# One joined product for four heads, scaling queued behind a split, spaced sums and an interleaved end in a hybrid mLSTM and sparse-attention block

## The chip, the cores and the metric

The kernel runs on one core of a Trainium2 chip. The metric is device time in microseconds (us) of one execution. Five engines have a queue of their own each and work through it in order: TensorE (PE, matrix products; its weight loads are listed apart as PEld), VectorE (DVE), ScalarE (ACT), GpSimd (POOL) and SyncE (SP, which issues most DMA transfers). They wait for each other by semaphores.

## The reference

One layer over 256 tokens of width 4096, batch 1, float32. Cut to what matters:

```python
h = _rmsnorm(x, norm_w)
u = h @ w_in                       # 4096 x about 15,400 columns
# mLSTM: 8 heads, from ml_q ml_k ml_v ml_o ml_z ml_i ml_f     -> y_ml
# sparse attention: 16 query heads in 4 groups of 4           -> y_ns
...
kcmp = _rmsnorm(_compress(kc), k_norm_w[0])     # 15 compressed keys per group
vcmp = _compress(vc)                            # 15 compressed values per group
p_c = _masked_softmax(q @ kcmp * scale + bias_c, dist_c >= 0)
o_c = p_c @ vcmp
o_s = ...   # attention over selected blocks (all 4 blocks of 64 here)
o_w = ...   # attention over a window
o = gs[..., 0:1] * o_c + gs[..., 1:2] * o_s + gs[..., 2:3] * o_w
...
x = x + concat([y_ml, y_ns]) @ w_out
x = x + sigmoid(x @ ple_gate) * (p @ ple_proj)
```

## The kernel before, in words

**Units.** The time goes to four big products with weights of 4096 rows: `w_in` (twice: `wide_group` for most columns, `pair_group` for gates), `w_out` and `ple_gate`. Weights arrive as `raw` tiles of 128x1024 over SP's queue. To keep float32 accuracy, each tile is split in two: ACT writes the high part `whi` (line 1315) and DVE the rest `wlo` (line 1316). PE then makes three products for each block, high by high, high by low and low by high. The work on one `raw` tile is a unit. In a `wide_group` a unit is 12 products of 512 columns (lines 819 and 821). The program's main loop over n emits, for unit n: the split of unit n+3 (`LOOK` = 3; four buffers each for `whi` and `wlo`), loads, PE's products of unit n, and then one step of a generator from the queue `urgent` and one from the queue `fifo`. All other work is written as such generators, so that a piece of it comes after each unit. `require(flag)` runs steps until a flag is set.

**Attention, `t_nq`.** It runs once for each of four groups, under the units of the first stage. After the compressed scores it goes through eight pairs (head h, token half t), one step of the loop to a unit. Three stages stand in a step, for pairs i, i-1 and i-2 and one older: `scores` (lines 489 to 491, PE, into a bank that is written anew in each step), `bias_max` (lines 500 and 502, DVE), `expo` (line 507, ACT), `coef` (lines 512 and 513, DVE), `scale` (line 517, ACT), `trans` (line 524, PE: two transposes where t is 0 and four where t is 1), `copy_pt` (line 529, DVE) and `pv` (line 535, PE). At the end of each `pv` one more product (line 538) adds the compressed branch: 15 rows of `pct` by 15 rows of `vcmp`, at row 32 times the head's number. That is 32 such products in the program.

**Mixed blocks.** `pair_group` has sixteen blocks kp of two `raw` tiles. Most are plain ("C"). Some are mixed: they save a product of eight by adding weights and activations first. The sums of weights are two DVE operations for each tile in `sums` (lines 1140 to 1144), and the sums of activations are made by `t_stat` for blocks 9, 11 and 13 and by `t_mix` (lines 698 to 711) for 3, 5 and 7. `t_mix` is used four times: twice early, and twice behind `t_stat`, in the first group of `w_out` (flag y) and the first group of `ple_gate` (flag r).

**The end.** The last group's four blocks of results (own, 128x512 each) are finished by `t_out_own`, g == 7: an add (line 1012, DVE), a sigmoid (line 1013, ACT), a product and an add (lines 1017 and 1018, DVE) and a DMA. The PE order `tail` lets these blocks be complete one after the other.

Of the kernel before, what the change touches and what calls it, by code (L numbers as in the profile page):

```python
# [13 lines left out]
AF = mybir.ActivationFunctionType  # L14
OP = mybir.AluOpType
# [6 lines left out]
NCMP = 15  # L22
# [51 lines left out]
def hymba_block(ctx: ExitStack, tc: tile.TileContext, a, out: bass.AP):  # L74
    nc = tc.nc
    MM = nc.tensor.matmul
# [14 lines left out]
    def side(i, shape):  # L91
        return psp.tile(shape, F32, tag=f"sd{i}", name=f"sd{i}")
# [4 lines left out]
    def sqtile(shape):  # L97
        return wk.tile(shape, F32, tag="sq", name="sq")

    def stile(shape):  # L100
        return wk.tile(shape, F32, tag="s", name="s", bufs=3)
# [4 lines left out]
    def small(shape, tag, bufs=2):  # L106
        return sm_.tile(shape, F32, tag=tag, name=tag, bufs=bufs)
# [44 lines left out]
    vcmp = wk.tile([128, 4, 128], F32, tag="vcmp", name="vcmp")  # L152
# [7 lines left out]


    fifo, urgent = deque(), deque()
    done = set()

    def step(queues=None):
# [250 lines left out]
    def t_nq(flag, g):  # L416
# [8 lines left out]
        for t in range(2):  # L425
            r = slice(t * 128, (t + 1) * 128)
# [18 lines left out]
        for t in range(2):  # L445
            for h in range(4):
                MM(pc[:, 4 * t + h, :], qt[:, h, t * 128:(t + 1) * 128], kct[:, g, :], start=True, stop=True)
        yield
        sc = small([128, 8, 32], "sc", 1)
        nc.gpsimd.memset(sc, 0.0)  # L450
        scv = sc[:, :, 0:NCMP]
# [16 lines left out]
        for t in range(2):  # L468
            nc.vector.tensor_tensor(scv[:, 4 * t:4 * t + 4], scv[:, 4 * t:4 * t + 4],
                                    mask01[:, t, None, :].to_broadcast([128, 4, NCMP]), op=OP.mult)  # L470
        yield
        pp = side(1, [128, 2, 128])
        for t in range(2):
            nc.tensor.transpose(pp[:, t, :], sc[:, 4 * t:4 * t + 4, :].rearrange("p h c -> p (h c)"), idn)
        yield
        pct = small([128, 2, 128], "pct", 1)
        nc.vector.tensor_copy(pct, pp)

        o = [side(2, [128, 4, 128]), side(3, [128, 4, 128])]
# [51 lines left out]
        def pv(i):  # L531
            h, t = units[i]
            for b in range(2):
                for s in range(t + 1):
                    MM(o[t][:, h, :], ptb[i][:, b, s, :], v[:, s, b, g * 128:(g + 1) * 128],
                       start=(b == 0 and s == 0), stop=False)

            MM(o[t][:, h, :], pct[32 * h:32 * h + NCMP, t, :], vcmp[32 * h:32 * h + NCMP, g, :],
               start=False, stop=True)

        def at(f, i):
            if 0 <= i < 8:
                f(i)

        for i in range(11):
            at(coef, i - 1)
            at(scale, i - 1)
            at(trans, i - 2)
            at(pv, i - 3)
            at(scores, i)  # L550
            at(copy_pt, i - 2)
            at(bias_max, i)
            at(expo, i)
            yield
        if g % 2 == 0:
            nat[2 + g // 2] = wk.tile([128, 2, 1024], F32, tag=f"nat{2 + g // 2}", name=f"y{2 + g // 2}")
        y = nat[2 + g // 2]
# [132 lines left out]
            t = held["cb"][:, int(kp == 11)]  # L690
        return t[:, 0], t[:, 1]

    def t_mix(kps, flag, early=False):

        f = {}
        for i in range(len(kps) + 1):
            if i:
                nc.vector.tensor_sub(cb[kps[i - 1]][1], f[i - 1], cb[kps[i - 1]][0])
                done.add(f"{flag}{kps[i - 1] // 2}m")
            if i == len(kps):  # L700
                return
            c, b = kps[i] // 2, 2 * (kps[i] % 2)
            v = f[i] = stile([128, 4, 128])
            nc.vector.tensor_add(v.rearrange("p a t -> p (a t)"), sh[c][:, b:b + 2].rearrange("p k t -> p (k t)"),
                                 sl[c][:, b:b + 2].rearrange("p k t -> p (k t)"))
            nc.vector.tensor_sub(v[:, 3:0:-2], v[:, 1::-1], v[:, 3:0:-2])
            nc.vector.tensor_sub(v[:, 0], v[:, 0], v[:, 3])
            nc.vector.tensor_sub(v[:, 2], v[:, 2], v[:, 0])
            yield
            cb[kps[i]] = mixed_tiles(kps[i], "a" if early else "b")  # L710
            nc.scalar.activation(cb[kps[i]][0], v, AF.Copy)
            yield

    def t_stat(chunks, weighted, bset=1, pace=2, pause=0):

# [123 lines left out]
    def add(*gens):  # L839
        fifo.extend(gens)  # L840
# [162 lines left out]
    def t_out_own(g, own, us, pj):  # L1003
        while f"mix{g}" not in done:
            yield
        x1 = nat[g - 4]
        if g == 7:
            for j in range(2):
                for t in range(2):
                    cs = (slice(0, 256), slice(256, 512)) if t and j else (slice(0, 512),)  # L1010
                    for c in cs:
                        nc.vector.tensor_add(us[j][:, t, c], own[t][j].t[:, c], us[j][:, t, c])  # L1012
                        nc.scalar.activation(us[j][:, t, c], us[j][:, t, c], AF.Sigmoid)  # L1013
                    for c in cs:
                        w, c0 = us[j][:, t, c], 512 - 512 * j + c.start
                        n = c.stop - c.start
                        nc.vector.tensor_tensor(w, w, pj[:, j, t, c], op=OP.mult)  # L1017
                        nc.vector.tensor_add(w, w, x1[:, t, c0:c0 + n])  # L1018
                        nc.sync.dma_start(out[t * 128:(t + 1) * 128, 3072 + c0:3072 + c0 + n], w)
            done.add("own7")  # L1020
            return
        for j in range(2):
            for t in range(2):
                nc.vector.tensor_add(us[j][:, t], own[t][j].t, us[j][:, t])
        done.add(f"own{g}")
        yield
        for j in range(2):
            u = us[j]
            nc.scalar.activation(u, u, AF.Sigmoid)
            nc.vector.tensor_tensor(u, u, pj[:, j], op=OP.mult)  # L1030
            yield
            c0 = 512 - 512 * j
            nc.vector.tensor_add(u, u, x1[:, :, c0:c0 + 512])
            nc.gpsimd.dma_start(out[:, (g - 4) * 1024 + c0:(g - 4) * 1024 + c0 + 512].rearrange("(t p) c -> p t c", p=128), u)
            yield
# [31 lines left out]
    def pair_group(g, w, stat):  # L1067
# [3 lines left out]
        own = [[Acc(6 * nC + (0 if (t, j) == (1, 0) else 3 * nM)) for j in range(2)] for t in range(2)]  # L1071
        oth = [Acc(3 * nM) for _ in range(4)]
        us, pj, raw, left, tail = [], {}, {}, {c: 2 for c in range(8)}, []
# [33 lines left out]
        def new_activations(g, chunks, b):  # L1107

            if g < 0:
                add(t_stat([(c, (c * 512 + 2048) % 4096, f"p1_{c}", f"y{c}") for c in chunks], range(16), b, pause=2 - 2 * b))  # L1110
            else:
                add(t_stat([(c, c * 512, f"p2_{c}", f"r{c}") for c in chunks], (), b, pause=2 - 2 * b))
            if b:
                add(t_mix((3, 5, 7), "y" if g < 0 else "r"))

        def finish(kp):
            if g in (-1, 3):
# [191 lines left out]
    def split_tiles():  # L1309
        return (wk.tile([128, 2, 512], F32R, tag="whi", name="whi", bufs=LOOK + 1),  # L1310
                wk.tile([128, 2, 512], F32R, tag="wlo", name="wlo", bufs=LOOK + 1))

    def split_all(r, keep=False):
        hi, lo = split_tiles()
        nc.scalar.activation(hi, r, AF.Copy)  # L1315
        nc.vector.tensor_sub(lo, r, hi)  # L1316
        held_raw[0] -= not keep
        return hi, lo
# [7 lines left out]
    def split(n):  # L1326
        r = raws.pop(n, None)
        if n == 0:
            hi, lo = split_tiles()
            for j in range(2):  # L1330
                split_x(j)
                nc.scalar.activation(hi[:, j], r[:, j], AF.Copy)
                nc.vector.tensor_sub(lo[:, j], r[:, j], hi[:, j])
            splits[n] = (hi, lo)
            held_raw[0] -= 1
            return
        if n < 16:
            split_x(2 * n)
            split_x(2 * n + 1)
        if n - 1 in XN:  # L1340
            done.add(f"xn{XN.index(n - 1)}")
        if units[n]["kind"] == "raw":
            splits[n] = (r, None)
        elif units[n]["kind"] == "narrow":
            hl = wk.tile([128, 8, 128], F32R, tag="whi", name="whl", bufs=LOOK + 1)
            nc.scalar.activation(hl[:, :, 0:64], r, AF.Copy)
            nc.vector.tensor_sub(hl[:, :, 64:128], r, hl[:, :, 0:64])
            splits[n] = (hl, None)
            held_raw[0] -= 1
        elif units[n]["kind"] == "pair":  # L1350
            splits[n] = units[n]["split"](r)
        else:
            splits[n] = split_all(r)
# [4 lines left out]
    def load_some():  # L1358
        while loads and held_raw[0] < RAWB:
            held_raw[0] += 1  # L1360
            load(loads.popleft())
# [6 lines left out]
    for n in range(N):  # L1368
        if n + LOOK < N:
            split(n + LOOK)  # L1370
        load_some()
        un = units[n]
        if un["pre"]:
            un["pre"]()
        un["mm"](*splits.pop(n))
        if un["kind"] == "raw":
            held_raw[0] -= 1
        if un["post"]:
            un["post"]()
        if n >= 3:  # L1380
            step([urgent])
            step([fifo])
# [85 lines left out]
```

## Time and profile before

| | |
|---|---|
| median of 3 runs | 2169.69 us (2169.62 to 2169.72) |
| the profiled execution | 2169.9 us, of which span 2168.1 us |
| PE | 2146.1 us busy, 99% of the span |
| PEld | 1756.3 us, 81% |
| DVE | 1565.5 us, 72% |
| ACT | 1152.1 us, 53% |
| POOL | 32.1 us, 1% |
| mean granted clock of TensorE | 0.999 |

The span runs from the first to the last instruction, and the profiled execution takes 1.8 us more than it. Shares are of the whole span. A busy PE may still be late: a product is counted as busy until its result has left the array, so the starts of products following each other are the finer measure. A float32 product appears as two MATMUL records, a transpose and a product of split parts as one.

### The profile page before, as it was taken

To read this page: it belongs to the slowest core of one execution; us is meant where nothing else is said; L and a number is where in the kernel's file an instruction comes from. 1 tells how busy PE (TensorE), PEld (TensorE's weight loads), DVE (VectorE), ACT (ScalarE), POOL (GpSimd) and SP (SyncE) were. 2 spreads that over 40 slices of the span, in tenths; PEclk is the share of its full clock that TensorE was granted. 3 is DMA by queue.
4 is the path that set the end of the run, shared out by engine and by line. 5 is a ranking of instruction groups with operands and counts; after the bars stand their busy time and mean duration, and the time that the engine had idled before them with its cause. 6 is when DMAs were issued, how large, how long until landed. Compare 5 with 4: busy or idle time off the path is not lost. (4 is left out here: it accounts for less than half of the span.)

```text
span 2168.1 us, 26804 instructions
## 1 busy us (share of the span) xinstructions
PE 2146.1 (99%) x9795; PEld 1756.3 (81%) x9795; DVE 1565.5 (72%) x1971; ACT 1152.1 (53%) x1462; POOL 32.1 (1%) x70
## 2 busy tenths in 40 slices
PE   9999999999999999999999999999999999999998
PEld 7876888787878788888888888887888888888887
DVE  6553555555555576658888888887898886888888
ACT  7543443545455555455555555565555555555554
POOL 1000000000000000000000000000000000000000
PEclk9999999999999999999999999999999999999999
DMA  9667665464645455655666666666675675666664
GB/s 380 200 196 264 192 188 181 127 186 127 186 133 166 139 184 173 195 167 193 185 196 224 183 200 213 197 204 218 205 229 180 202 226 160 205 196 223 204 217 141
DMA packets 118244, 422.08 MB, mean 195 GB/s; under 512 B 13650, under 2 KB 13962, under 8 KB 118112
## 3 DMA queue, kind: packets, MB, share of 16 engines
q1 hardware_dynamic: 114272, 409.00, 58.9%
q0 software_dynamic: 3696, 11.35, 1.7%
q8 instruction: 77, 1.26, 0.2%
q14 instruction: 55, 0.45, 0.1%
q10 hardware_dynamic: 144, 0.02, 0.0%
HBM read 416.08 MB, written 4.23 MB: 194 GB/s over the span
## 5 line engine op out<-in xcount | busy, mean ns | idle before, releaser
L1316 DVE TENSOR_TENSOR wlo<-raw,whi 128x1024 fp32r<-128x1024 f32 x818 | 998.0, 1223 | 537.3 <-ACT whi L1315 522.8
L1315 ACT ACTIVATE whi<-raw 128x1024 fp32r<-128x1024 f32 x818 | 863.4, 1060 | 789.2 <-PE mm L819 261.5
L819 PE MATMUL mm<-whi,sh 128*128 128x512 f32 x1152 | 362.3, 396 | 0.2 <-ACT whi L1315 0.2
L819 PE MATMUL mm<-whi,sl 128*128 128x512 f32 x1152 | 355.5, 390 | 0.0
L821 PE MATMUL mm<-wlo,sh 128*128 128x512 f32 x1152 | 355.4, 390 | 0.1
L821 PEld LDWEIGHTS mm<-wlo,sh 128*128 128x128 f32 x1152 | 216.1, 188 | 46.3 <-DVE wlo L1316 0.7
L819 PEld LDWEIGHTS mm<-whi,sl 128*128 128x128 f32 x1152 | 216.3, 188 | 46.0
L819 PEld LDWEIGHTS mm<-whi,sh 128*128 128x128 f32 x1152 | 210.6, 188 | 48.3 <-issue 5.9
L1064 PE MATMUL mm<-whi,sh 128*128 128x512 f32 x740 | 239.6, 392 | 2.5 <-DVE sl L759 1.9
L1064 PE MATMUL mm<-wlo,sh 128*128 128x512 f32 x740 | 237.1, 390 | 1.6 <-DVE wlo L1316 1.6
L1064 PE MATMUL mm<-whi,sl 128*128 128x512 f32 x740 | 236.9, 390 | 0.0
L1064 PE MATMUL sd<-whi,sh 128*128 128x512 f32 x677 | 219.8, 390 | 0.0
L1064 PE MATMUL sd<-whi,sl 128*128 128x512 f32 x677 | 219.4, 389 | 0.0
L1064 PE MATMUL sd<-wlo,sh 128*128 128x512 f32 x677 | 219.3, 389 | 0.0
L1064 PEld LDWEIGHTS mm<-wlo,sh 128*128 128x128 f32 x740 | 138.8, 188 | 31.1 <-DVE wlo L1316 2.2
L1064 PEld LDWEIGHTS mm<-whi,sh 128*128 128x128 f32 x740 | 137.8, 188 | 32.0 <-issue 3.5
L1064 PEld LDWEIGHTS mm<-whi,sl 128*128 128x128 f32 x740 | 139.0, 188 | 29.1
L1064 PEld LDWEIGHTS sd<-whi,sl 128*128 128x128 f32 x677 | 127.2, 188 | 26.6
L1064 PEld LDWEIGHTS sd<-wlo,sh 128*128 128x128 f32 x677 | 127.2, 188 | 26.5
L1064 PEld LDWEIGHTS sd<-whi,sh 128*128 128x128 f32 x677 | 126.8, 188 | 26.2
L1064 PE MATMUL mm<-whi,cb 128*128 128x512 f32 x318 | 103.9, 391 | 0.0
L1064 PE MATMUL sd<-whi,cb 128*128 128x512 f32 x282 | 94.3, 391 | 0.0
(301 smaller groups left out, 1677.6 us busy)
## 6 DMA issues: line engine op xcount, KB each, us to landing
raw<-in_w_in SPq DMA_DIRECT2D x287, 512.0 KB, 3.5
raw<-in_w_gate SPq DMA_DIRECT2D x192, 512.0 KB, 3.5
raw<-in_w_out SPq DMA_DIRECT2D x128, 512.0 KB, 3.8
raw<-in_ple_gate SPq DMA_DIRECT2D x128, 512.0 KB, 3.6
raw<-in_w SPq DMA_DIRECT2D x16, 512.0 KB, 3.5
u<-in_xt SPq DMA_DIRECT2D x16, 256.0 KB, 7.6
xn<-in_x SPq DMA_DIRECT2D x4, 1024.0 KB, 8.8
x<-in_x POOLq DMA_DIRECT2D x4, 1024.0 KB, 8.9
```

The source lines that it names most:

```text
L819: MM(box["ps"][t], s[c][:, k, t * 128:(t + 1) * 128], m[:, j, :], start=st, stop=False)
L821: MM(box["ps"][t], sh[c][:, k, t * 128:(t + 1) * 128], lo[:, j, :], start=False, stop=last)
L1064: MM(acc.t, s, m, start=acc.i == 0, stop=acc.i == acc.n - 1)
L1315: nc.scalar.activation(hi, r, AF.Copy)
L1316: nc.vector.tensor_sub(lo, r, hi)
```

## The change

Four edits:

1. In `t_nq`, the compressed values of the group's four heads are laid out as a block-diagonal tile `bd` of 128x512 (a GpSimd memset, and four ScalarE copies of 32x128 each). In step 2 of the loop one product for each token half, all 128 rows of `pct` by 512 columns of `bd`, opens the accumulation of all four heads. The 15-row product at the end of `pv` is gone.
2. The order within a step of `t_nq` is new: `scores` first, then `trans` and `pv`; `bias_max` ahead of `copy_pt`; `coef` for pair i in its own step, and `scale` for pair i put on a queue `behind`, which the main loop empties right after the next split.
3. `t_mix` takes a `gap`: with `gap=2`, used at the two later places, each of its yields becomes three.
4. In the end of the last group, the sum and the sigmoid of the next block are emitted ahead of the product, the add and the DMA of the one before.

```diff
@@ main loop
         if n + LOOK < N:
             split(n + LOOK)
+        while behind:
+            behind.popleft()()
         load_some()
@@ t_nq
+        bd = sqtile([128, 4, 128])
+        nc.gpsimd.memset(bd, 0.0)
         sc = small([128, 8, 32], "sc", 1)
...
+        for h in range(4):
+            r = slice(32 * h, 32 * h + 32)
+            nc.scalar.activation(bd[r, h, :], vcmp[r, g, :], AF.Copy)
         pp = side(1, [128, 2, 128])
...
                     MM(o[t][:, h, :], ptb[i][:, b, s, :], v[:, s, b, g * 128:(g + 1) * 128],
-                       start=(b == 0 and s == 0), stop=False)
-
-            MM(o[t][:, h, :], pct[32 * h:32 * h + NCMP, t, :], vcmp[32 * h:32 * h + NCMP, g, :],
-               start=False, stop=True)
+                       start=False, stop=(i == 6 + t and b == 1 and s == t))
...
         for i in range(11):
-            at(coef, i - 1)
-            at(scale, i - 1)
+
+            at(scores, i)
             at(trans, i - 2)
+            if i == 2:
+                for t in range(2):
+                    MM(o[t].rearrange("p h d -> p (h d)"), pct[:, t, :], bd.rearrange("p h d -> p (h d)"),
+                       start=True, stop=False)
             at(pv, i - 3)
-            at(scores, i)
+            at(bias_max, i)
             at(copy_pt, i - 2)
-            at(bias_max, i)
             at(expo, i)
+            at(coef, i)
+            if i < 8:
+                behind.append(lambda i=i: scale(i))
             yield
@@ t_mix
-    def t_mix(kps, flag, early=False):
+    def t_mix(kps, flag, early=False, gap=0):
...
-            yield
+            for _ in range(1 + gap):
+                yield
             cb[kps[i]] = mixed_tiles(kps[i], "a" if early else "b")
             nc.scalar.activation(cb[kps[i]][0], v, AF.Copy)
-            yield
+            for _ in range(1 + gap):
+                yield
...
-                add(t_mix((3, 5, 7), "y" if g < 0 else "r"))
+                add(t_mix((3, 5, 7), "y" if g < 0 else "r", gap=2))
@@ t_out_own, g == 7
+            parts = [(j, t, c) for j in range(2) for t in range(2)
+                     for c in ((slice(0, 256), slice(256, 512)) if t and j else (slice(0, 512),))]
+            for i in range(len(parts) + 1):
+                if i < len(parts):
+                    j, t, c = parts[i]
+                    nc.vector.tensor_add(us[j][:, t, c], own[t][j].t[:, c], us[j][:, t, c])
+                    nc.scalar.activation(us[j][:, t, c], us[j][:, t, c], AF.Sigmoid)
+                if i:
+                    j, t, c = parts[i - 1]
...
```

On DVE, a step of the loop in `t_nq` between two low parts (line 1316 before, 1330 after; `pt` is the copied transpose, `sd` a bank of PSUM, `s` the scores in SBUF, `sm` the coefficients). Before:

```order
L1316 TENSOR_TENSOR wlo<-raw,whi 128x1024
L512 RECIPROCAL sm_3095<-sm_3095 128x2
L513 TENSOR_TENSOR sm_3095<-sm_3095,sg 128x2
L529 COPY pt<-sd_3120 128x512
L500 TENSOR_TENSOR s<-sd_3128,tb 128x512
L502 TENSOR_REDUCE mx_3136<-s 128x2
L1316 TENSOR_TENSOR wlo<-raw,whi 128x1024
```

The same stretch of DVE's queue after the change:

```order
L1330 TENSOR_TENSOR wlo<-raw,whi 128x1024
L507 TENSOR_TENSOR s<-sd_3128,tb 128x512
L509 TENSOR_REDUCE mx_3141<-s 128x2
L536 COPY pt<-sd_3132 128x512
L519 RECIPROCAL sm_3145<-sm_3145 128x2
L520 TENSOR_TENSOR sm_3145<-sm_3145,sg 128x2
L1330 TENSOR_TENSOR wlo<-raw,whi 128x1024
```

The copy and the coefficients moved behind the row maximum, to just ahead of the next low part. On PE, the same step between two units (lines 819 and 821 before, 831 and 833 after, are the unit's products; `sd` are banks of PSUM). Before:

```order
L821 MATMUL mm_2742<-wlo,sh_460 128x512
L524 MATMUL sd_3120<-idn,s 128x128 x4
L535 MATMUL sd_3010<-vsw,pt 128x128 x2
L538 MATMUL sd_3010<-vcmp,pct 128x128
L489 MATMUL sd_3128<-kh,qh 128x512
L490 MATMUL sd_3128<-kh,ql 128x512
L491 MATMUL sd_3128<-kl,qh 128x512
L819 MATMUL mm_2741<-whi,sh_460 128x512
```

After:

```order
L833 MATMUL mm_2742<-wlo,sh_460 128x512
L496 MATMUL sd_3128<-kh,qh 128x512
L497 MATMUL sd_3128<-kh,ql 128x512
L498 MATMUL sd_3128<-kl,qh 128x512
L531 MATMUL sd_3132<-idn,s 128x128 x4
L542 MATMUL sd_3016<-vsw,pt 128x128 x2
L831 MATMUL mm_2741<-whi,sh_460 128x512
```

The scores moved ahead of the transposes, and the product of `vcmp` is gone (its successor, line 555, stands once for each half in step 2). ACT's order in these steps is what it was: exponentials, high part, scaling of the same pair. On DVE, in the first group of `w_out` around the second of the three sums of `t_mix` (lines 698 to 708 before, 708 to 718 after; 1140 to 1144 before and 1154 to 1158 after are sums of weights). Before:

```order
L1140 TENSOR_TENSOR raw<-raw 128x512
L1141 TENSOR_TENSOR raw<-raw 128x512
L698 TENSOR_TENSOR cb<-s,cb 128x512
L704 TENSOR_TENSOR s<-sh_11447,sl_11448 128x512
L706 TENSOR_TENSOR s<-s 128x2x128
L707 TENSOR_TENSOR s<-s 128x128
L708 TENSOR_TENSOR s<-s 128x128
L1316 TENSOR_TENSOR wlo<-raw,whi 128x1024
```

After:

```order
L1330 TENSOR_TENSOR wlo<-raw,whi 128x1024 x2
L1337 TENSOR_TENSOR wlo<-raw,whi 128x512
L708 TENSOR_TENSOR cb<-s,cb 128x512
L714 TENSOR_TENSOR s<-sh_11447,sl_11448 128x512
L716 TENSOR_TENSOR s<-s 128x2x128
L717 TENSOR_TENSOR s<-s 128x128
L718 TENSOR_TENSOR s<-s 128x128
L1330 TENSOR_TENSOR wlo<-raw,whi 128x1024 x2
```

The second sum moved from the middle of the first mixed block to the start of the second (line 1337 is that block's first low part); the third moved to the start of the third block.

## Rows read from the trace of the kernel before

**Rows 1.** Page, part 1: busy us (share of the span) and instructions of each engine
```profile
PE 2146.1 (99%) x9795; PEld 1756.3 (81%) x9795; DVE 1565.5 (72%) x1971; ACT 1152.1 (53%) x1462; POOL 32.1 (1%) x70
```

**Rows 2.** Waits, whole span: engine, line, releaser, total us, times, longest
```profile
PEld sd L524 <- ACT s L517: 14.9, 32, 1.1
```

**Rows 3.** Timeline of PE, a step with t = 0 transposed: start us, us
```profile
404.69 0.62 PE L821 MATMUL mm<-wlo,sh 128*128 128x512 f32 x2
405.16 0.38 PE L524 MATMUL sd<-idn,s 128*128 128x128 f32 x2
405.37 1.06 PE L535 MATMUL sd<-vsw,pt 128*128 128x128 f32 x8
406.36 0.48 PE L538 MATMUL sd<-vcmp,pct 15*128 15x128 f32 x2
406.77 0.39 PE L489 MATMUL sd<-kh,qh 128*128 128x256 f32 x1
407.00 0.28 PE L490 MATMUL sd<-kh,ql 128*128 128x256 f32 x1
```

**Rows 4.** Timeline of PE and PEld, the step before, with four transposes
```profile
398.93 0.61 PE L821 MATMUL mm<-wlo,sh 128*128 128x512 f32 x2
...
399.99 0.20 PEld L524 LDWEIGHTS sd<-idn,s 128*128 128x128 f32 x2 [0.87 <-ACT s L517]
399.99 0.84 PE L524 MATMUL sd<-idn,s 128*128 128x128 f32 x4 [0.45 <-ACT s L517]
...
400.39 0.20 PEld L524 LDWEIGHTS sd<-idn,s 128*128 128x128 f32 x2 [0.20 <-ACT s L517]
...
400.66 0.61 PE L535 MATMUL sd<-vsw,pt 128*128 128x128 f32 x4
...
401.20 0.48 PE L538 MATMUL sd<-vcmp,pct 15*128 15x128 f32 x2
```

**Rows 5.** Timeline of PE: float32 products of 257 columns in the mLSTM
```profile
806.43 0.59 PE L642 MATMUL sd<-mv,pt 128*128 128x257 f32 x2
806.86 0.60 PE L643 MATMUL sd<-mv,pt 128*128 128x257 f32 x2
```

**Rows 6.** Timeline of DVE, two steps of attention
```profile
415.13 0.68 DVE L500 TENSOR_TENSOR s<-sd,tb 128x512 f32<-128x512 f32 x1
...
418.70 1.23 DVE L1316 TENSOR_TENSOR wlo<-raw,whi 128x1024 fp32r<-128x1024 f32 x1 [2.17 <-ACT whi L1315]
419.84 0.16 DVE L512 RECIPROCAL sm<-sm 128x2 f32<-128x2 f32 x1
...
420.45 0.41 DVE L500 TENSOR_TENSOR s<-sd,tb 128x256 f32<-128x256 f32 x1
...
424.41 0.16 DVE L512 RECIPROCAL sm<-sm 128x2 f32<-128x2 f32 x1
...
425.28 0.68 DVE L500 TENSOR_TENSOR s<-sd,tb 128x512 f32<-128x512 f32 x1
```

**Rows 7.** Waits of PE between 1500 and 1525 us
```profile
PE mm L1064 <- DVE wlo L1316: 1.8, 2, 1.6
PE sd L1064 <- DVE wlo L1316: 1.5, 1, 1.5
```

**Rows 8.** Timeline of DVE: a sum of activations, and later a block's slack
```profile
1504.09 0.69 DVE L698 TENSOR_TENSOR cb<-s,cb 128x512 fp32r<-128x512 f32 x1
...
1506.40 1.22 DVE L1316 TENSOR_TENSOR wlo<-raw,whi 128x1024 fp32r<-128x1024 f32 x1
...
1575.53 2.54 DVE L1316 TENSOR_TENSOR wlo<-raw,whi 128x1024 fp32r<-128x1024 f32 x2 [0.83 <-ACT whi L1315]
```

**Rows 9.** Timeline of the end, all engines
```profile
2160.14 0.39 PE L1064 MATMUL sd<-wlo,sh 128*128 128x512 f32 x1
...
2162.81 0.75 DVE L1012 TENSOR_TENSOR u<-sd,u 128x256 f32<-128x256 f32 x2
...
2164.96 0.42 DVE L1018 TENSOR_TENSOR u<-u,x 128x256 f32<-128x256 f32 x1
```

More of the change, by code (lines that the diff above doesn't have):

```diff
@@ L162, in hymba_block @@
     fifo, urgent = deque(), deque()
+    behind = deque()
     done = set()
@@ L1007, in t_out_own @@
         if g == 7:
[L1008 to L1019, printed above, removed]
+            parts = [(j, t, c) for j in range(2) for t in range(2)
[7 more added lines that the diff above has]
+                    j, t, c = parts[i - 1]
+                    w, c0 = us[j][:, t, c], 512 - 512 * j + c.start
+                    n = c.stop - c.start
+                    nc.vector.tensor_tensor(w, w, pj[:, j, t, c], op=OP.mult)
+                    nc.vector.tensor_add(w, w, x1[:, t, c0:c0 + n])
+                    nc.sync.dma_start(out[t * 128:(t + 1) * 128, 3072 + c0:3072 + c0 + n], w)
             done.add("own7")
```

## The prediction, made before the change was timed

> **What bounds the kernel now.** The page's list of engines comes first: PE is busy for 99% of the span [rows 1]. So only two things can save time: PE work that goes away, and starts of products that are late. The timeline of PE shows both, and the reader is to look at starts, since a product's end runs under the next one's start. The waits then name who is late, and in attention one wait stands out: the weight loads of the transposes, 14.9 us for ACT's scaling [rows 2]. The timelines of DVE say why.
>
> **Part 1, the joined product.** Take the price of one 15-row product. Eight records of `pv` ahead of it span 0.99 us [rows 3] and four span 0.54 us [rows 4]; the difference is 0.1125 for each, so 0.09 is an extra at the border to the 15-row product. The product itself lasts 0.41 from start to start (406.36 to 406.77) [rows 3] and 0.42 (401.20 to 401.62, where its successor starts). The first product behind it shows 0.39 where its like shows 0.28, 0.11 more [rows 3]. That is 0.61 us, 32 times: 19.5 us go. I take nothing for what the last `pv` will cost ahead of the unit that now follows it; no row shows that border, and it lies between 0 and the 0.11 of the border named, 3.5 us in all.
>
> In return come eight products of 512 columns, in two records each. The nearest row is 257 columns in float32 with all 128 rows: 0.43 us for two records [rows 5], hence 0.43 x 512 / 257 = 0.86 for the product, 6.9 us for eight. The trade gives 19.5 - 6.9 = **12.6 us** (9 with the border). The memset and the sixteen copies stand on POOL and ACT two steps ahead of use, where neither is what PE waits for; uncovered, a group's four copies of about 0.4 us would cost 1.6 us, so 6 us for all.
>
> One rule speaks against this. The Trainium skill, "TensorE: Matmul & The Clock Gate", section "Step-by-step: what each phase is for", says that the time of a weight load follows the number of columns and that the row count does not matter. By it a 15-row product would cost what a full one does, two records of 0.1125, and the trade would give 32 x 0.225 - 6.9 = 0.3 us. The rows above show 0.61. "TensorEngine Tiling (Array Packing)", section "Key Properties", agrees with them: a change of tiling mode drains the engine.
>
> **Part 2, the order in attention.** In a step with four transposes, start to start from the unit's last pair is 1.06 us [rows 4] against 0.47 in a step with two [rows 3], and the four take 0.84 against 0.38 + 0.21: lost 0.59 + 0.25 = 0.84 us, while the two weight loads waited 0.87 + 0.20 = 1.07. So 0.23 of a step's waits are hidden. Sixteen such steps: 14.9 - 16 x 0.23 = **11.2 us** lost.
>
> Why the scaling is late: it needs `coef`, which stands on DVE behind the low part, which waits for the high part, which follows the exponentials on ACT. DVE idles 2.17 us ahead of that low part [rows 6]. After the change `coef` and the copy fill this idle time, and the scaling runs a step ahead of its transposes. The new wait is `coef` for the exponentials, with the low part queued behind it; but that part waits for the high part anyway, and ACT starts the high part only when the exponentials are done (about 1.1 us more).
>
> Will the chain of DVE and ACT still hold PE? It goes from the add of scores (line 500) through maximum, exponentials, high part and low part to the next add. Before, a pair of steps takes 415.13 to 425.28, 10.15 us. Without coefficients and copy, the rows give 415.13 to 419.84 and 420.45 to 424.41: 4.71 + 3.96 = 8.67 us [rows 6]. PE's own work for a pair: two units of 12 products at 0.23 (0.62 for two records less 0.39 for one [rows 3, 9]), 5.5; scores 0.35 and 0.69; six transposes at 0.105, 0.63; twelve records of `pv`, 1.35; together 8.5. So the chain falls back by 0.15 us in a pair, 0.6 in a group, and in two groups the evacuation of `mv` adds about 1.2. It must fall back about 2 us before PE is held at the banks of scores and transposes, since the bank of a pair is needed again a step of over 4 us later and is read within about 2 us. I take no new wait, with 4 us as the worst of this (1 us for each group).
>
> **Part 3, sums of activations.** PE waits 1.8 + 1.5 = 3.3 us for low parts between 1500 and 1525 [rows 7], with late weight loads some 3.7. A piece of `t_mix` costs DVE 1504.09 to 1506.40, 2.31 us [rows 8], and three fall into the first mixed block. A mixed block leaves DVE 0.83 us idle [rows 8] of PE's 10.2. Spread, each of the second and third blocks begins with a piece: DVE falls back 2.31 - 0.83 = 1.5 us in each. The waits of before show what the lookahead absorbs: 3 x 2.31 - 0.83 = 6.1 behind for 3.7 waited, so 2.4. Spread, the opening piece (1.7, since 0.6 of each 2.31 closes the one before) leaves 0.9 in the first block, so it comes to 0.9 + 1.5 + 1.5 = 3.9 at the third, 3.9 - 2.4 = 1.5 to 1.8 waited. Gain **2.0 us**, between 0 (the debt is only later, and then collides with the block's end) and 3.7. The second use (flag r) waits for nothing now and has two units of another kind ahead of it; I take nothing there.
>
> **Part 4, the end.** PE's last product ends at 2160.53; its block's first add starts at 2162.81, and the last DVE operation ends at 2165.38 [rows 9]. In the new order the adds of the earlier blocks are done by then; behind PE stand the half block's add (0.4), product and add of the block before (2 x 0.68 [rows 6] with issue 1.4), then the second half's add and two products and adds (0.35 + 4 x 0.42 = 2.05): 2160.58 + 3.85 = 2164.4. Gain **0.95 us**, nothing if the DMA ends last anyway, since the last transfer is as long.
>
> **The sum.** 12.6 + 11.2 + 2.0 + 0.95 = 26.8 us. From the profiled execution, 2169.9 us: 2143.1. The median of the runs is 0.2 below that execution, so 2142.9 us.
>
> **The rivals.**
> A. The chain binds attention: coefficients and copy are not hidden in DVE's idle time, the pair stays at 10.15. Then PE loses (10.15 - 8.5) x 16 = 26 us less 2 us absorbed in each of four groups, 18: 2161. A half-hidden one gives about 2150. For it: the chain is at 8.67 against 8.5, with nothing to spare. Against: the idle time is 2.17 and what moves into it 0.3 + 0.7.
> B. The full-row price holds: 0.3 instead of 12.6, 2155. Only the border seen in rows 3 and 4 being an artefact of the record would bring it.
> C. Slower: `coef` holds DVE, so that low parts come late for the unit three ahead. That decides when a pair of steps takes 8.5 + (26.8 + 8) / 16 = 10.7 us, 2 us above the chain worked out; at 11 it would give 2175. Its place would be waits of PE for the low part in attention, where there are none now.
> D. Spacing gives nothing, or the wait moves behind the block: 2145. E. Nothing changes, because what is saved returns as waits elsewhere: 2169.
>
> **How the numbers follow.** Forecast, with D and the border of part 1 (2140 to 2147): 0.76. A in full or part (2147 to 2161): 0.12. B: 0.06. E: 0.03. C: 0.03. The range leaves out the full A, B, E and C and takes in the half-hidden chain: 2139.5 to 2150; below, all of part 3 and 1 us more. Faster by over 0.2% (4.3 us, about what a measurement can tell from no change) 0.95; within it 0.03; slower 0.02.
>
> **What the profile after would show.** No row of 15 rows; a row of 128x512 with `pct`, sixteen records about 0.43 apart. No weight load of the transposes waiting for the scaling, and the step's starts 4.0 to 4.6 us apart. DVE's idle time ahead of low parts in attention near 1 us instead of 2.17. Waits for low parts near 1516 and 1528 instead of 1508 and 1514, halved. The last DVE operation 3.9 us behind PE's last product, not 4.9. Wrong would be: waits of PE for `s`, `sd` banks or low parts in attention (A, C), or products behind `pv` that start 0.1 late.

## The result, and the profile after

The changed kernel takes 2143.8 us (median of 4 runs, 2142.94 to 2144.05) against 2169.65 for the kernel before (4 runs, 2169.57 to 2169.72): a ratio of 0.988, with a 95% interval of 0.9863 to 0.9897. The profiled execution took 2142.94 us, its span 2141.2.

Part 1 of the page after the change answers to [rows 1]. PE has 48 records fewer: 64 of the 15-row products went, 16 of the joined ones came.

```profile
PE 2127.5 (99%) x9747; PEld 1749.5 (82%) x9747; DVE 1568.4 (73%) x1971; ACT 1153.3 (54%) x1478; POOL 33.8 (2%) x74
```

The waits after the change (engine, line, releaser, total us, times, longest) answer to [rows 2, 7]. Line 531 holds the transposes, line 1078 the products of `w_out` and `ple_gate`.

```profile
PEld sd L531 <- ACT s L514: 1.2, 3, 0.4
...
PE mm L1078 <- DVE sl L771: 1.9, 2, 1.0
PE mm L1078 <- DVE wlo L1330: 1.3, 2, 0.9
PE sd L1078 <- DVE wlo L1330: 0.6, 2, 0.4
```

The 14.9 us for ACT's scaling are gone. Three weight loads of transposes still wait, and over the whole span PE waits four times for low parts, 1.9 us (before five times, 3.6).

The timeline of PE answers to [rows 3, 4]: first the step in which the joined products run, then a step with four transposes and one with two (start us, us).

```profile
395.61 0.38 PE L531 MATMUL sd<-idn,s 128*128 128x128 f32 x2
395.83 1.88 PE L555 MATMUL sd<-sq,pct 128*128 128x512 f32 x4
397.15 1.03 PE L831 MATMUL mm<-whi,sh 128*128 128x512 f32 x2
...
400.31 0.39 PE L496 MATMUL sd<-kh,qh 128*128 128x512 f32 x1
...
404.64 0.28 PE L496 MATMUL sd<-kh,qh 128*128 128x256 f32 x1
...
405.22 1.06 PE L542 MATMUL sd<-vsw,pt 128*128 128x128 f32 x8
406.03 0.71 PE L831 MATMUL mm<-whi,sh 128*128 128x512 f32 x2
406.58 0.62 PE L831 MATMUL mm<-whi,sl 128*128 128x512 f32 x2
...
408.87 0.39 PE L496 MATMUL sd<-kh,qh 128*128 128x512 f32 x1
```

`sq` on line 555 is the buffer of `bd`. Four of its records take 1.32 us to the next start, and the product behind them takes 1.03 where its like takes 0.62: 1.32 + 0.41 = 1.73, or 0.43 for a record and 6.9 us for sixteen. From `pv` to the second row of the unit (each row is two products) it is 405.22 to 406.58, 1.36 us. The steps start 4.33 and 4.23 us apart, 8.56 for a pair.

The timeline of DVE answers to [rows 6]: the same two kinds of step, with the idle time ahead of an instruction in brackets.

```profile
414.68 1.23 DVE L1330 TENSOR_TENSOR wlo<-raw,whi 128x1024 fp32r<-128x1024 f32 x1 [0.58 <-ACT whi L1329]
415.82 0.42 DVE L507 TENSOR_TENSOR s<-sd,tb 128x256 f32<-128x256 f32 x1
416.27 0.42 DVE L509 TENSOR_REDUCE mx<-s 128x2 f32<-128x256 f32 x1
416.61 0.41 DVE L536 COPY pt<-sd 128x256 f32<-128x256 f32 x1
417.70 0.17 DVE L519 RECIPROCAL sm<-sm 128x2 f32<-128x2 f32 x1 [0.68 <-ACT s L514]
...
418.65 1.23 DVE L1330 TENSOR_TENSOR wlo<-raw,whi 128x1024 fp32r<-128x1024 f32 x1 [0.59 <-ACT whi L1329]
...
423.37 1.23 DVE L1330 TENSOR_TENSOR wlo<-raw,whi 128x1024 fp32r<-128x1024 f32 x1 [0.59 <-ACT whi L1329]
```

The 2.17 us ahead of a low part have become 0.59, with 0.68 more ahead of the reciprocal; copy and coefficients fill the rest. A pair takes 414.68 to 423.37, 8.69 us instead of 10.15.

In the first group of `w_out` and of `ple_gate` the timelines answer to [rows 7, 8]. The first two rows are DVE's (a sum of activations, now at a block's start), the others PE's waits.

```profile
1485.80 0.69 DVE L714 TENSOR_TENSOR s<-sh,sl 128x512 f32<-128x512 f32 x1
...
1487.51 2.35 DVE L1330 TENSOR_TENSOR wlo<-raw,whi 128x1024 fp32r<-128x1024 f32 x2
```

```profile
1488.79 0.50 PE L1078 MATMUL mm<-wlo,cb 128*128 128x512 f32 x1 [0.35 <-DVE wlo L1330]
...
1500.21 0.50 PE L1078 MATMUL mm<-wlo,cb 128*128 128x512 f32 x1 [0.90 <-DVE wlo L1330]
...
1847.33 0.50 PE L1078 MATMUL sd<-wlo,cb 128*128 128x512 f32 x1 [0.38 <-DVE wlo L1330]
```

The end answers to [rows 9]. DVE now ends at 2138.48, 3.7 us behind PE's 2134.78; before it was 4.9.

```profile
2134.39 0.39 PE L1078 MATMUL sd<-wlo,sh 128*128 128x512 f32 x1
...
2134.82 0.42 DVE L1025 TENSOR_TENSOR u<-sd,u 128x256 f32<-128x256 f32 x1 [0.70 <-PE sd L1078]
...
2138.06 0.42 DVE L1032 TENSOR_TENSOR u<-u,x 128x256 f32<-128x256 f32 x1
```

To see where the time went, cut the span at products that both kernels have. These are PE's rows of after: the first compressed scores, the first product of the mLSTM's `mqk`, the first transposes of `y` and of `x`, and the first product of `ple_proj`.

```profile
373.06 1.85 PE L448 MATMUL sd<-kct,sq 128*128 128x15 f32 x16
...
769.99 0.59 PE L627 MATMUL sd<-mqk 128*128 128x256 f32 x2
...
1413.37 0.60 PE L736 MATMUL mm<-idn,y 128*128 128x128 f32 x4
...
1758.23 0.60 PE L736 MATMUL mm<-idn,x 128*128 128x128 f32 x4
...
1874.54 0.39 PE L1239 MATMUL mm<-whi,ph 128*128 128x512 f32 x1
```

| stretch, us | before | after | difference |
|---|---|---|---|
| start, to the first compressed scores | 373.87 | 373.06 | -0.81 |
| attention, to the first `mqk` | 419.88 | 396.93 | -22.95 |
| to the first transpose of `y` | 643.36 | 643.38 | 0.02 |
| first part of `w_out`, to the first transpose of `x` | 347.30 | 344.86 | -2.43 |
| first part of `ple_gate`, to the first `ph` | 115.88 | 116.31 | +0.43 |
| rest, to PE's last end | 260.24 | 260.24 | 0 |
| tail, to the end of the span | 7.53 | 6.39 | -1.13 |

The differences add up to the 26.9 us between the spans. The 0.81 of the start isn't the change's: that stretch is the same program, and it lies between 373.06 and 374.38 over the profiled runs of this study. Without it 26.1 us are left, and the medians differ by 25.85.

### The profile page after: what moved, and what is told of

The parts are those of the page before. It is cut to its first block, busy times and chain, and to the rows that moved or that the text cites. A ratio compares the mean times of both kernels' runs of the same rounds, so it can differ in the third digit from the quotient of the medians.

```text
span 2141.2 us, 26729 instructions
## 1 busy us (share of the span) xinstructions
PE 2127.5 (99%) x9747; PEld 1749.5 (82%) x9747; DVE 1568.4 (73%) x1971; ACT 1153.3 (54%) x1478; POOL 33.8 (2%) x74
## 3 DMA queue, kind: packets, MB, share of 16 engines
HBM read 416.08 MB, written 4.23 MB: 196 GB/s over the span
```

## The experiments

The kernel before was measured beside all of them, at 2169.61 to 2169.79. "Attention" is that stretch of the table above, in the profiled run.

| kernel | median, us (range) | ratio to before (95%) | attention, us |
|---|---|---|---|
| joined product alone | 2165.22 (2164.36 to 2165.92) | 0.9979 (0.997 to 0.9988) | 415.18 |
| order in attention alone | 2159.1 (2159.06 to 2159.15) | 0.9951 (0.9934 to 0.9967) | 409.16 |
| all but the joined product | 2156.14 (2155.53 to 2156.29) | 0.9937 (0.9922 to 0.9951) | 409.13 |
| the same, 32 rows | 2155.48 (2155.07 to 2156.18) | 0.9935 (0.9923 to 0.9948) | 409.15 |
| 32 full-row products | 2145.82 (2145.61 to 2146.19) | 0.989 (0.9875 to 0.9905) | 399.26 |
| both kinds | 2149.92 (2149.43 to 2150.11) | 0.9909 (0.9893 to 0.9924) | 403.09 |
| DVE's order as before | 2162.59 (2161.85 to 2162.85) | 0.9967 (0.9955 to 0.998) | 415.19 |
| PE's order as before | 2144.15 (2143.61 to 2144.44) | 0.9883 (0.9869 to 0.9896) | 397.89 |
| no spacing | 2145.5 (2145.39 to 2145.75) | 0.9889 (0.9876 to 0.9903) | 396.95 |
| spacing in `w_out` alone | 2143.6 (2143.25 to 2143.84) | 0.988 (0.9867 to 0.9894) | 396.94 |
| wider spacing, in `w_out` alone | 2141.5 (2141.36 to 2141.78) | 0.9871 (0.9855 to 0.9886) | 397.01 |
| end as before | 2145.02 (2144.32 to 2145.34) | 0.9886 (0.9873 to 0.99) | 396.88 |

Two theories stood at the start. One takes the edits as a sum: each has its price on PE and is worth it alone. The other says that the chain of DVE and ACT sets attention's pace, so that PE's work is worth nothing until the chain is shorter. Diffs are against the changed kernel.

**The joined product alone.** Edits 2 to 4 are undone; the diff shows the order (edit 2).

```diff
         for i in range(11):
-
-            at(scores, i)
+            at(coef, i - 1)
+            at(scale, i - 1)
             at(trans, i - 2)
...
             at(pv, i - 3)
-            at(bias_max, i)
+            at(scores, i)
             at(copy_pt, i - 2)
+            at(bias_max, i)
             at(expo, i)
-            at(coef, i)
-            if i < 8:
-                behind.append(lambda i=i: scale(i))
```

> The kernel before with the joined product alone (edit 1); order, sums and end as before. Theory of the chain: ScalarE and VectorE set the pace of attention before, 10.15 us a pair of steps, so PE work taken away comes back as longer waits of the transposes; about 2167 us, between 2165 and 2170. Rival, prices add up: 12.6 us less, 2157 us. The waits of weight loads for the scaling tell which: well above 14.9 us by the first, about 14.9 by the second.

It gained 4.6 us, not 12.6. Its waits and two of its DVE rows say why.

```profile
PEld sd L530 <- ACT s L523: 23.0, 31, 1.9
...
PE sd L530 <- ACT s L523: 11.0, 9, 1.4
```

```profile
412.36 1.22 DVE L1323 TENSOR_TENSOR wlo<-raw,whi 128x1024 fp32r<-128x1024 f32 x1 [1.90 <-ACT whi L1322]
...
422.51 1.22 DVE L1323 TENSOR_TENSOR wlo<-raw,whi 128x1024 fp32r<-128x1024 f32 x1 [1.96 <-ACT whi L1322]
```

The pair still takes 10.15 us, to the hundredth what it took before [rows 6], though PE has 12.6 us less to do. Most of what PE no longer does, it waits: 23.0 us instead of 14.9 at the same weight loads, so 8.1 of the 12.6 came back, and the other 4.5 agree with the gain. The chain theory held in the main, though PE's work was worth more than nothing.

**The order alone.** Edit 2 is kept, the 15-row products are back, and the sums and the end are as before; the diff shows the products.

```diff
-                       start=False, stop=(i == 6 + t and b == 1 and s == t))
+                       start=(b == 0 and s == 0), stop=False)
+
+            MM(o[t][:, h, :], pct[32 * h:32 * h + NCMP, t, :], vcmp[32 * h:32 * h + NCMP, g, :],
+               start=False, stop=True)
...
-            if i == 2:
-                for t in range(2):
-                    MM(o[t].rearrange("p h d -> p (h d)"), pct[:, t, :], bd.rearrange("p h d -> p (h d)"),
-                       start=True, stop=False)
```

> The kernel before with the new order in attention alone (edit 2); the 15-row products stay. Chain: 8.67 us a pair against 9.7 of PE, so PE sets the pace and the 11.2 us of late transposes go, 2158.5 us. Rival, the order only pays together with the joined product (something else holds the transposes): above 2165 us.

Attention is 10.7 us shorter and no transpose waits. Alone, the two edits take 4.7 and 10.7 us from attention, 15.4 together; in the changed kernel they take 22.95. The joined product is worth its price only where the order lets PE run.

**All but the joined product; 32 rows instead of 15; 32 full-row products.** The first keeps edits 2 to 4 and goes back to the 15-row products by the diff just shown. The second takes slices of 32 rows in them; the third takes all 128 rows of `pct` by one head of `bd`, so that there are as many products as before, none on a part of the rows. Of the last two only the new product is shown.

```diff
+            MM(o[t][:, h, :], pct[32 * h:32 * h + 32, t, :], vcmp[32 * h:32 * h + 32, g, :],
+               start=False, stop=True)
```

```diff
+            MM(o[t][:, h, :], pct[:, t, :], bd[:, h, :], start=False, stop=True)
```

> The changed kernel with the 15-row products back in place of the joined one (edits 2, 3 and 4 without 1; the block-diagonal tile is still made). Price from the rows, 0.61 us each against 6.9 in all for the joined ones: 12.6 us more, 2156.4 us. Rival, full-row price (0.225 each): 0.3 us more, 2144.1 us.

> As the run with 15-row products in the new order (2156.1 us), but over the 32 rows of the head, 17 of them zeros. If the price is that of any product on a part of the rows: 2156.1 us. If it falls with the rows used: towards 2145.8 us, the run with 128 rows.

> The changed kernel with one product a head as before, but over all 128 rows: pct by the 128 columns of that head in the block-diagonal tile, 32 products of 128 columns in place of 8 of 512. If the 15 rows are what costs 0.61 us: 32 x 0.225 = 7.2 against 6.9 us, so 2144.1 us. If the number of products or their place at the end of pv costs: 2156 us, as with 15 rows.

PE's timeline with 15 rows, and then with all rows, in the step with eight records of `pv`:

```profile
405.30 1.06 PE L542 MATMUL sd<-vsw,pt 128*128 128x128 f32 x8
406.29 0.48 PE L545 MATMUL sd<-vcmp,pct 15*128 15x128 f32 x2
406.70 0.72 PE L830 MATMUL mm<-whi,sh 128*128 128x512 f32 x2
407.27 0.63 PE L830 MATMUL mm<-whi,sl 128*128 128x512 f32 x2
```

```profile
404.54 0.41 PE L531 MATMUL sd<-idn,s 128*128 128x128 f32 x2 [0.30 <-ACT s L514]
404.79 1.06 PE L542 MATMUL sd<-vsw,pt 128*128 128x128 f32 x8
405.68 0.39 PE L545 MATMUL sd<-sq,pct 128*128 128x128 f32 x2
405.82 0.71 PE L829 MATMUL mm<-whi,sh 128*128 128x512 f32 x2
406.37 0.62 PE L829 MATMUL mm<-whi,sl 128*128 128x512 f32 x2
```

From `pv` to the unit's second row it is 1.97 us with 15 rows, 1.58 with all rows, and 1.36 without either (after the change, above). So the 15-row product costs 0.61 us and the full-row one 0.22. With 32 rows attention takes 409.15, within 0.02 of the 15 rows' 409.13. The weight loads of the same two products show part of the reason, with 15 rows and then with all:

```profile
406.29 0.29 PEld L545 LDWEIGHTS sd<-vcmp,pct 15*128 15x128 f32 x2
406.70 0.30 PEld L830 LDWEIGHTS mm<-whi,sh 128*128 128x128 f32 x2
```

```profile
405.57 0.30 PEld L545 LDWEIGHTS sd<-sq,pct 128*128 128x128 f32 x2
```

With all rows the first load starts 0.11 us ahead of its product (405.57 and 405.68), while `pv` still runs. With 15 rows it starts only with its product (406.29), and the unit's first load behind it only with the unit (406.70). The Trainium skill ("TensorE: Matmul & The Clock Gate", "Step-by-step: what each phase is for") says that the time of a weight load does not depend on the row count. For the load alone the trace agrees: 0.29 and 0.30 us for two. The products are not alike for that: fewer rows cost 0.39 us more, at 15 and at 32 alike.

The full-row kernel is 2.0 us slower than the changed one, though 32 x 0.22 and 6.9 are nearly equal. Its transposes wait, as the row at 404.54 shows. The label names ACT's exponentials. But those of the pair that is transposed had been done since 400.3, and its scaling since 401.8; the one that ends at 404.40 is of the next pair, which these transposes don't read. What they need, and what ends just ahead, is DVE's copy of the pair before, which frees the one bank that they write.

```profile
402.39 0.68 DVE L507 TENSOR_TENSOR s<-sd,tb 128x512 f32<-128x512 f32 x1
...
403.71 0.68 DVE L536 COPY pt<-sd 128x512 f32<-128x512 f32 x1
403.89 0.51 ACT L514 ACTIVATE s<-s,mx 128x256 f32<-128x256 f32 x1 [2.09 <-PE mm L831]
```

The copy ends at 404.39. Either these products stand in a bad place, or the late transposes come from PE being too far ahead of the chain in a group's first steps, where nothing is transposed yet; then the joined products in step 2 give the chain time to catch up.

**Both kinds.** The full-row kernel, with the joined products of step 2 added again; their result is overwritten by the first `pv`, so they only take time.

```diff
-                       start=False, stop=(i == 6 + t and b == 1 and s == t))
+                       start=(b == 0 and s == 0), stop=False)
+
+            MM(o[t][:, h, :], pct[:, t, :], bd[:, h, :], start=False, stop=True)
...
-                       start=True, stop=False)
+                       start=True, stop=True)
```

> The run with 32 full-row products (2145.8 us), and the two joined products a group put back in step 2 as idle work whose result is overwritten. Theory: PE runs ahead of the chain in steps 0 to 2, which have few products, and the joined product at step 2 takes up that lead; without it the transposes wait for their bank, 2 us in all. Then the idle work costs 6.9 us and saves 2.0: 2150.7 us, and PE's waits of the transposes (1.2 us there) are gone. Rival, the 32 products themselves make the transposes wait: 2152.7 us, waits as they were.

The 6.9 us of products cost 4.1 us (2149.92 - 2145.82), and no transpose waits. The lead explains also why the waits of the full-row kernel shrink along a group (0.30 us at 404.5, 0.13 at 413.8). So work in step 2 comes back in part: the place of the joined products is worth some 2 to 3 us beside their price. Whether another early place would do as well, no run shows.

**DVE's order as before, and PE's order as before.** Edit 2 taken apart, with edits 1, 3 and 4 kept.

```diff
             at(scores, i)
+            at(coef, i - 1)
+            at(scale, i - 1)
             at(trans, i - 2)
...
-            at(bias_max, i)
             at(copy_pt, i - 2)
+            at(bias_max, i)
             at(expo, i)
-            at(coef, i)
-            if i < 8:
-                behind.append(lambda i=i: scale(i))
```

```diff
-            at(scores, i)
             at(trans, i - 2)
...
             at(pv, i - 3)
+            at(scores, i)
             at(bias_max, i)
```

> The changed kernel with the scores first on PE, but coefficients, copy and scaling of the older pairs ahead of the add of scores on VectorE, as before. If VectorE's order is what shortens the chain: 10.15 us a pair again, some 18 us lost, 2160 us (2155 to 2165), with waits of the transposes back. If PE's order (scores first) is what helps: 2144 us.

> The changed kernel with PE's order in a step as before (transposes, joined product, pv, then scores) and VectorE's order new. If VectorE's order alone shortens the chain: 2143.8 us. If the scores' place counts too, as the add of scores then comes later in the step: some waits come back, 2145 to 2149 us.

With DVE's old order the kernel takes 2162.6, and its pair is 10.15 again:

```profile
413.04 1.23 DVE L1329 TENSOR_TENSOR wlo<-raw,whi 128x1024 fp32r<-128x1024 f32 x1 [1.89 <-ACT whi L1328]
...
423.19 1.23 DVE L1329 TENSOR_TENSOR wlo<-raw,whi 128x1024 fp32r<-128x1024 f32 x1 [1.95 <-ACT whi L1328]
```

Here the scores wait too, for DVE's add that frees their bank (line 496; line 531 holds the transposes):

```profile
PE sd L496 <- DVE s L507: 7.3, 12, 1.0
PE sd L531 <- ACT s L524: 5.7, 4, 1.4
```

With PE's old order attention loses 1.0 us, at seven late weight loads instead of three; the medians differ by 0.35 and their ranges overlap, so only the stretch shows it. So nearly all of edit 2 is where coefficients, scaling and copy stand, and which of these three counts most no run tells; that the scores go first on PE is worth about 1 us.

**The spacing.** None; in `w_out` alone; and five yields instead of three in `w_out`, none more in `ple_gate`.

```diff
-                add(t_mix((3, 5, 7), "y" if g < 0 else "r", gap=2))
+                add(t_mix((3, 5, 7), "y" if g < 0 else "r"))
```

```diff
-                add(t_mix((3, 5, 7), "y" if g < 0 else "r", gap=2))
+                add(t_mix((3, 5, 7), "y" if g < 0 else "r", gap=2 * (g < 0)))
```

```diff
-                add(t_mix((3, 5, 7), "y" if g < 0 else "r", gap=2))
+                add(t_mix((3, 5, 7), "y" if g < 0 else "r", gap=4 * (g < 0)))
```

> The changed kernel with the sums of activations not spaced (edits 1, 2 and 4). By the traces spacing gains 2.4 us in the first group of w_out and loses 0.55 in the first group of ple_gate: 1.9 us more, 2145.7 us. If the waits only move: 2143.8 us.

> The changed kernel with the sums spaced in the first group of w_out alone. The one wait of 0.4 us (0.55 with the late weight load) near 1847 us goes: 2143.2 us. Rival, that wait was there anyway: 2143.8 us.

> The same with each yield made five instead of three in the first group of w_out: the third sum then falls behind the mixed blocks. By the debt of VectorE, 0.9, then 2.4, then 1.6 us, never above the 2.4 that the lookahead takes: the remaining 1.6 us of waits near 1489 and 1500 go too, 2141.7 us. Rival, the debt is then paid at the sums of the results behind the blocks: 2143 us.

Without spacing the waits of before are back: 1.7 and 1.7 us for `wlo`, 2145.5. With spacing in `w_out` alone the wait at 1847 is gone from the trace and that stretch is back at 115.87; the median, 0.2 lower, is too near to show it by itself. With the wider spacing the waits for low parts are all but gone:

```profile
PE sd L1078 <- DVE wlo L1330: 0.2, 1, 0.2
PE mm L1078 <- DVE wlo L1330: 0.2, 1, 0.2
```

These two stand at 976 and 979, ahead of `w_out`, where the kernel before has them too. The first part of `w_out` takes 343.11 instead of 344.86, and the kernel 2141.5, 2.3 us less than the changed one (0.5 of it from `ple_gate`) and the fastest of the study; the ranges don't touch.

**The end as before.** The new loop over `parts` goes back to the two nested ones.

```diff
-            parts = [(j, t, c) for j in range(2) for t in range(2)
...
+            for j in range(2):
+                for t in range(2):
+                    cs = (slice(0, 256), slice(256, 512)) if t and j else (slice(0, 512),)
```

> The changed kernel with the end as before (edits 1 to 3). By the traces, PE's end to the span's end was 7.52 us and is 6.39: 1.1 us more, 2144.9 us. If the last transfer ends last anyway: 2143.8 us.

The tail is 7.54 us again, and the median 1.2 above the changed kernel's.

## Why the prediction was right, and where its terms were off

The median is 0.9 us above the forecast of 2142.9.

**Part 1 (12.6) held in size.** The 15-row product costs the predicted 0.61 us, the joined ones the predicted 6.9 us. The border behind `pv` that could have cost 3.5 costs nothing: with the unit behind it, 405.22 to 406.58 is 1.36 us, eight records of `pv` at 0.1125 (0.90) and two unit products at 0.23, with nothing between them. Taking the joined product out again cost 12.3 us by the medians (2156.14 - 2143.8), 12.2 in attention. What the sum did not say is that this term depends on part 2: alone it gives 4.6, because with DVE's old order the chain of rival A binds.

**Part 2 (11.2) held, with the stated cause.** Alone the order gave 10.7. The chain worked out at 8.67 us for a pair is 8.69, PE's own 8.5 is 8.56. The idle time ahead of low parts is 0.59, foretold near 1, with 0.68 more ahead of the reciprocal. "I take no new wait" nearly held: three weight loads wait 1.2 us in all, and the three starts they hold are 0.17 to 0.19 late, 0.55 together. Both parts were to give 23.8 and gave 22.95; 0.55 of the 0.85 that is missing is these starts, which the kernels with the new order and 15-row products don't show. The rest is in the order, which alone gave 0.5 less than its 11.2; the joined product without the late starts would have given 0.2 more than 12.6 (12.23 in attention, and 0.55).

The late starts are in the three groups in which DVE, between two steps, also copies a block of `mv` or `u` out of its bank, 0.66 us each (at 406.5, 511.0 and 615.5); the fourth group has none of either. The prediction reckoned with two such groups at 1.2 us, and with about 2 us by which the chain may fall back before PE is held. Measured it falls back by 0.13 in a pair and 0.66 once, some 1.2 in a group, and PE is held: the 2 us were too much.

The step left out, and the likely reason for that, is the lead of PE in a group's first steps, where only scores run and no transpose holds it to the chain. The sum prices the joined products by their length alone; their place in step 2 takes up part of that lead, as the full-row kernels show. With nearly the same work in `pv` the time is 2 us more (2145.8).

**Part 3 (2.0) held as a sum of two errors, so the agreement of the total is luck.** `w_out` gained 2.43, and the use with flag r lost 0.43, where "I take nothing" was the step that failed: a wait of 0.38 us that was not there before. The waits stand in the second and third mixed blocks as worked out, but at 1488.8 and 1500.2, where the times foretold, less the 23 us saved ahead of them, would be 1493 and 1505. They are 0.35 and 0.90 instead of one wait of 1.5 to 1.8: the debt is worked off in two places.

**Part 4 (0.95)** measures 1.13 in the tail and 1.2 by its own experiment. DVE ends 3.7 us behind PE, foretold 3.9.

**The rivals.** A, the chain that binds, fell for this kernel but not as a mechanism: with DVE's old order it is there, at 2162.6 where A's working gave 2161. B, the full-row price, fell: 0.61 against 0.22. C: there is no wait for low parts in attention, and the pair would have had to be 2 us longer than 8.69. D fell: without spacing 2145.5, 1.7 above the changed kernel. E, savings that return as waits elsewhere, fell: 2143.8 against its 2169.

## What to carry to other kernels

When two engines run at nearly the same pace (here 8.56 and 8.69 us a pair, 10.15 before), work taken off one of them is worth its price only once the other has been shortened: cost such edits together, and work out both paces for each. Small operations that a later step needs belong into the idle time that their engine spends waiting anyway, ahead of the wait's end, not behind it. A sum that fills an engine's slack is spread until the lookahead hides it whole (four more yields here, not two), and only where it waits today.

## What was not expected of the hardware

- A float32 product on 15 or on 32 rows costs 0.61 us where the same on 128 rows costs 0.22: 0.09 ahead of it, 0.41 itself and 0.11 behind it, with 15 and 32 rows alike. It is dear also where the slice begins at row 0 (0.42, the first head's, in rows 4). The Trainium skill, "TensorEngine Tiling (Array Packing)", "Key Properties", says that a change of tiling mode drains the engine; the 0.09 and 0.11 at the borders, and the weight loads that start late there, agree with that, if a product on part of the rows counts as such a change, which no run here shows; the longer product itself is not explained by it. Its further statement that tiles work independently, in parallel, could show nothing here, where one such product runs at a time. No run has a number of rows between 32 and 128, and the full-row products also read another tile (`bd` for `vcmp`).
- A wait's label can name the wrong engine when two instructions end together: the transposes at 404.54 stood behind DVE's copy out of their one bank (to 404.39), not behind ACT's exponential (to 404.40), which belongs to another pair.
- The first 373 us, the same program in all these kernels, differ by up to 1.3 us between profiled runs (373.06 to 374.38), more than some of the terms measured here. Terms of about 1 us are read from stretches, not from totals.
